# Row factors from transposed tiles, and first results held on chip, in a hybrid encoder layer

## The chip, the cores and the metric

The kernel runs on one core of a Trainium2 chip. The metric is the device time of one execution in microseconds; of several runs the median counts. The core has five engines that work side by side and wait for one another by semaphores: TensorE (PE in the profile, with its weight loads as PEld), VectorE (DVE), ScalarE (ACT), GpSimd (POOL) and SyncE (SP). SP issues nearly all DMA transfers in its program order; ACT and POOL issue a few.

## The reference, cut to what matters

```python
def hybrid_layer(x, w_in, w_out, norm_w, ...):          # x: 1 x 1024 x 2048, float32
    h = rms_norm(x, norm_w)                             # x * rsqrt(mean(x*x) + 1e-6) * norm_w, per token
    proj = h @ w_in                                     # 2048 x 6656
    rq, rk, rv, rg, aq, ak, av, ag = jnp.split(proj, splits, axis=-1)
    y_ret = retention_branch(rq, rk, rv, ...) * jax.nn.silu(rg)
    y_att = window_attention_branch(aq, ak, av, sink) * jax.nn.silu(ag)
    return x + jnp.concatenate([y_ret, y_att], axis=-1) @ w_out

def reference(...):
    return rms_norm(hybrid_layer(...), final_norm_w)
```

For the change only the beginning matters: `h = rms_norm(x)` and the first blocks of `h @ w_in`. The factor of a token needs the sum of squares over all 2048 columns of its row of `x`.

## The kernel before

**The projection.** All products are computed in a split form: each float32 operand is taken as a rounded high part and a remainder (`split`, `operand`, `low`: the high part is a cast on ScalarE, the remainder a subtraction on VectorE, line 86), and three matmuls (`mm3`, lines 100 to 102) make one product. The weights stand as stationary operands, 128 x 128; the transposed activations stream, 512 tokens at a time. `w_in` is worked off in blocks of 512 columns (`BLOCKS`), in two halves of the 2048 rows (`part` 0 and 1), in the order of `PHASES`. Inside a block with its 1024 rows of `w_in` the work is a two-by-two product of quarters in seven products instead of eight (`PRODUCTS`), whose operands are sums and differences of quarters: `w_next` and `mixed` make those of the weights, `sum_of` and `put` those of the activations, in `comb[i]`.

**The opening.** The first three blocks of part 0 are `akv`, `aq0` and `aq1`. They begin before the row factors are known. `plain` computes block `akv` with four ordinary quarters, first for token half 0 from `x` scaled by `norm_w` alone; then `early` computes one quarter of `aq0` and one of `aq1`, also for token half 0; then `plain` computes `akv` for token half 1, with factors; then `rest` does the remaining products of `aq0` and `aq1`. After that the ordinary loop goes on with `rk0`. The results that were made without factors, eight tiles of 128 x 512 (four from `plain`, two from each `early`), are stored unscaled to `pr` in HBM (lines 372 to 377 and 399 to 404) and noted in `unscaled`. The job `rescaled` (lines 1186 to 1196) later loads them back two at a time into `ct` buffers (line 1191), multiplies them by the row of factors (line 1194) and stores them again.

**The factors.** `src0` holds the transposed tiles of x's first 1024 columns, `[128, s, k, token]`, s = 0, 1 and k = 0 to 3, loaded by `load_first`. The squares don't use it: `load_rows` and `load_row_beside` load x's eight blocks of 128 rows in natural layout, 1 MiB each, and `square` sums the squares of half a row at a time, eleven halves on ScalarE (line 501) and five on VectorE (line 503). `factors_of` adds both halves and raises to the power -0.5 on POOL (line 510), `spread` repeats the result over 128 columns (line 1075), and `turn_rows` transposes that on TensorE (line 1079) and copies it into `both`, whose halves are `rows_of` (line 1080). `scale` multiplies a tile of `src0` by `norm_w` and that row (line 1084).

**What sets the order.** Each call of `advance` is a step: six matmuls are emitted, and then every running job moves on by one `yield`. Steps 1 to 16 are `plain` for token half 0, 17 to 24 `early` of `aq0`, 25 to 32 `early` of `aq1`, 33 to 48 `plain` for half 1, 49 to 68 `rest` of `aq0`, 69 to 88 `rest` of `aq1`, and `rk0` begins with step 89. The job `opening` performs what the dictionary `plan` lists for each step (`at(n, what, ...)`, lines 1131 to 1178). TensorE, SP and POOL keep program order throughout; up to step 66 (`BY_HAND`) the others do too, and afterwards a planner orders VectorE and ScalarE, except for what `behind` pins. `flush` sends the collected stores to SP at every fourth step. `keep` stores the operands of part 0 to HBM for a later phase, `second_part` loads and scales the transposed tiles of x's other 1024 columns into the buffer of `src0`.

**Buffers that matter.** `ct` is a ring of eight tiles of 128 x 512, used for every result between its bank and its store. `pj` and `ax` are four PSUM banks each. The tag `tt` has four tiles of 128 x 1024. The `a11` to `a22` tiles hold weight quarters, and `c1` to `c7` operands and, early on, natural rows.

Of the kernel before, what the change touches and what calls it, by code (L numbers as in the profile page):

```python
# [38 lines left out]
M = 4  # L39
# [20 lines left out]
def hybrid_layer_kernel(  # L60
# [293 lines left out]
    def plain(b, m, of, ops_):  # L354

        for n, k in QUARTERS:
# [5 lines left out]
            for q in range(M):  # L362
# [7 lines left out]
                if last:  # L370
                    for a in range(2):
                        e = ct()
                        nc.scalar.copy(out=e, in_=banks[a])
# [18 lines left out]
    def early(b):  # L392
# [84 lines left out]
    junk = st.tile([P, 2, PART], BF16, name="junk", tag="tt", bufs=4)  # L477
    ssx = st.tile([P, 2, NT], F32, name="ssx")
    natural = {}

    def load_rows(slot, *tokens):

        both = combp.tile([P, 2, 2, PART], F32, name="xt", tag=f"c{slot}")
        for i, t in enumerate(tokens):
            natural[t] = both[:, i, 0], both[:, i, 1]
            nc.sync.dma_start(out=both[:, i], in_=x[blk(t)].rearrange("p (h c) -> p h c", h=2))

    def load_row_beside(t):

        natural[t] = [st.tile([P, PART], F32, name="xh", tag="tt", bufs=4) for _ in range(2)]  # L490
        for i in range(2):
            nc.sync.dma_start(out=natural[t][i], in_=x[blk(t), i * PART:(i + 1) * PART])
# [4 lines left out]
    def square(t, i, act):  # L497

        of = natural[t][i]
        if act:  # L500
            nc.scalar.activation(out=junk[:, 0], in_=of, func=AF.Square, accum_out=ssx[:, i, t:t + 1])
        else:
            nc.vector.tensor_tensor_reduce(out=junk[:, 1], in0=of, in1=of, scale=1.0, scalar=0.0,
                                           op0=ALU.mult, op1=ALU.add, accum_out=ssx[:, i, t:t + 1])
# [544 lines left out]
    w_next[1, 1] = quarter(*u1, 1, 1)  # L1049
    load_rows(6, 4, 5)  # L1050
    w_next[1, 2] = quarter(*u1, 1, 2)
    load_rows(7, 6, 7)
    load_first(nc.sync, 0, 1)
    early_w = {1: st.tile([P, M, 2 * P], F32, name="b", tag="tt", bufs=4), 2: wp.tile([P, M, 2 * P], F32, name="s2", tag="s2")}

    def early_quarter(k):
        nc.sync.dma_start(out=early_w[k], in_=w_at((k - 1) * M, BLOCKS[u2[1]]))

    early_quarter(1)
    load_first(nc.sync, 1, 1)  # L1060

    def load_rest():
        load_rows(6, 0, 1)
        early_quarter(2)
        load_row_beside(2)
        for n in (2, 1), (2, 2):
            w_next[n] = quarter(*u1, *n)
# [18 lines left out]
    def hold_second():  # L1086
        t = combp.tile([P, 2, M, HALF], F32R, name="b12", tag="c7")
        quarters[1, 1] = t[:, 0], t[:, 1]
        hold(3, 0)
# [28 lines left out]

    mixed_first = mixed(w_next, then_of(1))
# [11 lines left out]
    at(6, lambda: ready.append(operand(w_next[1, 1])))  # L1131
    for n, t in ((9, 4), (11, 5), (14, 6), (16, 7)):
        at(n, square, t, 0, True)
        at(n, square, t, 1, False)
    at(12, load_rest)
    at(13, lambda: ready.append(operand(w_next[1, 2])))
    at(16, factors_of, 4, 8)
    at(17, spread, 1)
    at(20, lambda: turn_rows(1, first_banks[0, 2][0]))
    at(20, lambda: ready.append(operand(early_w[1])))  # L1140
    at(20, hold_second)
    at(20, second_half, 0, "scale")
    for k in range(2 * M):
        at(21 + k, second_half, k, "high")
        if k + 1 < 2 * M:
            at(21 + k, second_half, k + 1, "scale")
        at(21 + k, second_half, k, "low")
    for n, t, i in ((23, 0, 0), (24, 0, 1), (25, 1, 0), (25, 1, 1), (27, 2, 0), (28, 2, 1), (31, 3, 0)):
        at(n, square, t, i, True)
    at(25, lambda: ready.append(operand(early_w[2])))  # L1150
    at(26, load_rows, 6, 3)
    at(31, square, 3, 1, False)
    at(31, factors_of, 0, 4)
    at(33, spread, 0)
    for n in (29, 30, 32, 32, 34, 43, 51, 52, 56, 60):
        at(n, step)
    at(35, lambda: turn_rows(0, first_banks[u1[1], 2][0]))
    for k in range(M):
        at(36 + k // 2, scale, 0, k, 0)
    for j in range(2):  # L1160
        at(38 + j, sum_of, 5, j)
        at(40 + j, sum_of, 6, j)
        at(42 + j, put, 5, j)
        at(45 + j, put, 6, j)
        at(47 + j, sum_of, 7, j)
        at(48 + j, scale, 1, 2 * j, 0)
        at(48 + j, scale, 1, 2 * j + 1, 0)
        at(50 + j, put, 7, j)
        at(51 + j, sum_of, 4, j)
        at(54 + j, put, 4, j)  # L1170
        at(57 + j, put, 1, j)
        at(62 + j, put, 2, j)
    for n, i in ((40, 5), (43, 6), (48, 7), (52, 4)):
        at(n, hold, i, 0)
    at(41, first_scaled, u1[1])
    at(62, lambda: start(keep(0)))
    at(66, lambda: start(second_part()))
# [8 lines left out]
    def rescaled():  # L1186
# [463 lines left out]
```

## Time and profile before

| what | value |
|---|---|
| median of three runs | 1524.88 us (1523.79 to 1527.82) |
| profiled execution | 1520.95 us, its span 1519.1 us |
| mean granted TensorE clock | 0.993 |
| ScalarE busy | 670.6 us, 44% of the span |
| HBM read, written | 202.21 MB, 129.24 MB |
| DMA packets | 142228, 324.39 MB |

A row of the timeline gives start, duration, engine, source line, operation, output and inputs, the shapes, the count of merged instructions, and in brackets the idle time before the first of them with what ended it. Times are microseconds from the start of the span. `SPq` and `ACTq` are DMA issues: the duration is that of the issue, not of the transfer. A matmul's duration includes its way through the pipeline, so the distance of starts tells the rate. The granted clock is 1.00 at full speed.

### The profile page before, as it was taken

How to read it: one execution, taken by the hardware profiler on the slowest of the kernel's cores; microseconds unless marked ns; L12 is line 12 of the kernel's file. 1: busy time of each engine (PE TensorE's matmuls, PEld its weight loads, DVE VectorE, ACT ScalarE, POOL GpSimd, SP SyncE). 2: the span in 40 equal slices, each digit the busy share in tenths (PEclk: the TensorE clock that was granted, in tenths of full speed). 3: DMA queues.
4: the chain of work that ended last, by engine and by line, in shares of the span. 5: the costliest groups of instructions: out<-in, count | busy, mean ns of one | idle time of the engine just before them, and what ended most of it. 6: DMA issues, size and time to landing. Idle time of an engine off the chain costs nothing.

```text
span 1519.1 us, 19942 instructions
## 1 busy us (share of the span) xinstructions
PE 1485.2 (98%) x7096; PEld 1246.9 (82%) x7096; DVE 1117.3 (74%) x1932; ACT 670.6 (44%) x1091; POOL 149.2 (10%) x176
## 2 busy tenths in 40 slices
PE   9998999999999999999999999999999999999997
PEld 8777788888888888888888788887888878888886
DVE  4897595557858685867988899887655966776766
ACT  5531263234535453533434445354444663542425
POOL 0000001111110000001211100001211102020001
PEclk9999999999999999999999999999999999999999
DMA  9539776888675535798877766589787799495656
GB/s 372 182 121 390 251 249 187 227 223 251 165 235 195 169 123 190 273 339 185 176 185 167 176 178 187 172 293 325 224 233 194 175 210 211 90 205 175 211 179 250
DMA packets 142228, 324.39 MB, mean 214 GB/s; under 512 B 31664, under 2 KB 52528, under 8 KB 132400
## 3 DMA queue, kind: packets, MB, share of 16 engines
q1 hardware_dynamic: 118224, 272.23, 53.6%
q0 software_dynamic: 19728, 36.71, 16.4%
q10 hardware_dynamic: 4176, 14.17, 2.7%
q8 instruction: 56, 0.92, 0.2%
q14 instruction: 44, 0.36, 0.1%
HBM read 202.21 MB, written 129.24 MB: 218 GB/s over the span
## 4 chain that ended last, share of the span: by engine, by line
PE 75%; issue 9%; DMA 8%; DVE 5%; ACT 1%; POOL 1%; SPq 0%; ACTq 0%; POOLq 0%; DVEq 0%
PE pj L102 19%; PE pj L100 18%; PE pj L101 18%; PE ax L101 5%; PE ax L102 5%; PE ax L100 5%; PE ax L875 2%; PE ax L662 1%; DMA src<-in_x_f_dram 1%; DMA pr<-ct 1%; DVE wL L86 1%; DMA c<-kept 1%; DMA a<-in_w_in_dram 1%; DMA ysrc<-pr 1%; PE ax L926 1%
## 5 line engine op out<-in xcount | busy, mean ns | idle before, releaser
L100 PE MATMUL pj<-c,wH 128*128 128x512 f32 x1384 | 550.8, 398 | 10.7 <-DVE ct L93 5.3
L102 PE MATMUL pj<-c,wL 128*128 128x512 f32 x1384 | 543.9, 393 | 9.5 <-DVE wL L86 9.4
L101 PE MATMUL pj<-c,wH 128*128 128x512 f32 x1384 | 541.5, 391 | 0.0
L102 PEld LDWEIGHTS pj<-c,wL 128*128 128x128 f32 x1384 | 261.3, 189 | 70.1 <-DVE wL L86 14.6
L100 PEld LDWEIGHTS pj<-c,wH 128*128 128x128 f32 x1384 | 261.6, 189 | 61.9 <-issue 6.5
L101 PEld LDWEIGHTS pj<-c,wH 128*128 128x128 f32 x1384 | 261.7, 189 | 49.4
L86 DVE TENSOR_TENSOR wL<-a,wH 128x1024 fp32r<-128x1024 f32 x151 | 183.9, 1218 | 111.1 <-ACT wH L194 61.1
L194 ACT CAST wH<-a 128x1024 fp32r<-128x1024 f32 x121 | 127.1, 1050 | 181.6 <-PE pj L101 137.0
L336 ACT COPY ct<-pj 128x512 f32<-128x512 f32 x184 | 107.0, 586 | 191.9 <-PE pj L102 186.5
L93 DVE TENSOR_TENSOR ct<-pj,ct 128x512 f32<-128x512 f32 x170 | 112.6, 684 | 51.5 <-PE pj L102 42.1
L309 POOL DMA_DIRECT2D pr<-ct x88 | 78.1, 963 | 522.5 <-DVE ct L93 411.8
L86 DVE TENSOR_TENSOR wL<-s,wH 128x1024 fp32r<-128x1024 f32 x57 | 69.6, 1221 | 58.5 <-ACT wH L194 51.8
L101 PE MATMUL pj<-wL,c 128*128 128x512 f32 x224 | 87.3, 390 | 0.5 <-DVE wL L86 0.5
L102 PE MATMUL pj<-wH,c 128*128 128x512 f32 x224 | 87.2, 389 | 0.0
L100 PE MATMUL pj<-wH,c 128*128 128x512 f32 x224 | 87.1, 389 | 0.0
L101 PE MATMUL ax<-wL,c 128*128 128x512 f32 x208 | 81.2, 390 | 0.6 <-DVE wL L86 0.6
L102 PE MATMUL ax<-wH,c 128*128 128x512 f32 x208 | 81.0, 389 | 0.0
L100 PE MATMUL ax<-wH,c 128*128 128x512 f32 x208 | 80.9, 389 | 0.0
L194 ACT CAST wH<-s 128x1024 fp32r<-128x1024 f32 x51 | 53.6, 1051 | 16.2 <-PE pj L101 8.6
L89 ACT CAST wH<-a 128x1024 fp32r<-128x1024 f32 x28 | 29.5, 1054 | 62.1 <-PE pj L102 35.0
L652 ACT ACTIVATE s<-s,nm 128x385 f32<-128x385 f32 (+1 forms) x64 | 37.6, 588 | 30.1 <-DVE nm L647 27.2
L101 PEld LDWEIGHTS pj<-wL,c 128*128 128x128 f32 x224 | 42.0, 188 | 9.7 <-DVE wL L86 0.9
(227 smaller groups left out, 2121.0 us busy)
## 6 DMA issues: line engine op xcount, KB each, us to landing
a<-in_w_in_dram SPq DMA_DIRECT2D x103, 512.0 KB, 5.9
kept<-c SPq DMA_DIRECT2D x28, 1024.0 KB, 7.3
c<-kept SPq DMA_DIRECT2D x28, 1024.0 KB, 8.9
pr<-ct SPq DMA_DIRECT2D x96, 256.0 KB, 5.7
pr<-ct POOLq DMA_DIRECT2D x88, 256.0 KB, 5.9
a<-in_w_out_dram SPq DMA_DIRECT2D x18, 512.0 KB, 4.9
rx<-pr SPq DMA_DIRECT2D x64, 128.0 KB, 5.5
ysrc<-pr ACTq DMA_DIRECT2D x16, 512.0 KB, 6.4
```

The costliest lines, as they stand in the source:

```text
L86: return nc.vector.tensor_tensor(out=dst, in0=src, in1=high.bitcast(F32), op=ALU.subtract)
L89: behind(pinned, nc.scalar.copy(out=dst_h, in_=src))
L93: nc.vector.tensor_tensor(out=dst, in0=a, in1=b, op=ALU.add)
L100: nc.tensor.matmul(po, aH, bH, start=first, stop=False, **kw)
L101: nc.tensor.matmul(po, aH, bL, start=False, stop=False, **kw)
L102: nc.tensor.matmul(po, aL, bH, start=False, stop=last, **kw)
L194: behind(pinned, nc.scalar.copy(out=wH, in_=src))
L309: nc.gpsimd.dma_start(out=dst, in_=t, accum_op=ALU.add)
L336: nc.scalar.copy(out=t, in_=bank)
L652: nc.scalar.activation(out=s[:, 0:w + 1], in_=s[:, 0:w + 1], func=AF.Exp, scale=-1.0, bias=nm, accum_out=den)
L662: nc.tensor.transpose(pt[:, blk(j)], s[:, blk(j)], ident)
L875: nc.tensor.matmul(p, k_tok[:, c // 2, :, c % 2], vd[:, c, d], start=True, stop=True)
```

## The change

- **First loads.** The first piece of `src0` goes to SP's queue as its first transfer and the small vectors become the first on ACT's; both halves of the first weight quarter are on SP.
- **Squares of the first 1024 columns** come from `src0`. `square_columns` squares two 512-wide tiles at a time on ScalarE into the four `tt` tiles, `add_columns` sums them on VectorE, and `sum_columns` sums over the partitions with eight matmuls of one column against a tile of ones, then copies four columns of sums to `ssx`.
- **Squares of the other 1024 columns** still come from natural rows, of which only that half is loaded now (`load_row`, 512 KB each); all eight are on ScalarE (`square_row`), in steps 13 to 22.
- **Results without factors** stay in their `ct` buffers. `scale_result` multiplies two at a time in steps 28, 31, 37 and 48 and hands them to the stores. The first store, the load back and the second store of `rescaled` are gone.
- **The plan** is shifted: the factors of token half 0 are made in step 23 instead of 31 and turned in step 26 instead of 35; the early weight quarters use the tags `a21` and `a22`, so the two quarters of `aq0` that belong there are loaded in steps 21 and 25; operands 7, 4 and 2 are placed later; `second_part` starts in step 69 instead of 66.

The diff, cut to its core:

```diff
@@ plain, early @@
-                        stores.append((True, to, e))
-                        if m == 0:
-                            unscaled.append(to)
+                        (unscaled if m == 0 else stores).append((True, to, e))
...
-            stores.append((True, to, e))
-            unscaled.append(to)
+            unscaled.append((True, to, e))
@@ squares @@
-    junk = st.tile([P, 2, PART], BF16, name="junk", tag="tt", bufs=4)
+    junk = wp.tile([P, PART], BF16, name="junk", tag="ct", bufs=8)
+    columns = [st.tile([P, 2, HALF], F32, name="xx", tag="tt", bufs=4) for _ in range(4)]
...
+    def load_row(t):
+        nc.sync.dma_start(out=natural[t], in_=x[blk(t), PART:])
...
+    def square_row(t):
+        nc.scalar.activation(out=junk, in_=natural[t], func=AF.Square, accum_out=ssx[:, 1, t:t + 1])
+
+    def square_columns(m, i):
+
+        s, j = divmod(i, 2)
+        nc.scalar.activation(out=columns[(m, 2, 3, 2)[i]], in_=src0[:, s, 2 * j:2 * j + 2, half(m)], func=AF.Square)
+
+    def add_columns(m, i):
+        acc = columns[m]
+        if i < 4:
+            add(acc, acc, columns[(m, 2, 3, 2)[i]])
         else:
...
+            add(acc[:, 0], acc[:, 0], acc[:, 1])
+
+    def sum_columns(m, pt):
+
+        for t in range(4):
+            nc.tensor.matmul(pt[:, t:t + 1], columns[m][:, 0, blk(t)], ones, start=True, stop=True)
+        nc.vector.tensor_copy(out=ssx[:, 0, 4 * m:4 * m + 4], in_=pt[:, 0:4])
@@ first loads @@
+    load_first(nc.sync, 0, 0, 0, 1)
+    nc.scalar.dma_start(out=vec_t, in_=vecs)
     half_of_a11(nc.sync, 0)
-    load_first(nc.scalar, 0, 0, 0, 1)
-    nc.scalar.dma_start(out=vec_t, in_=vecs)
     load_first(nc.sync, 0, 0, 1, 1)
-    half_of_a11(nc.scalar, 2)
+    half_of_a11(nc.sync, 2)
...
+    def early_quarter(k):
+        t = early_w[k] = wp.tile([P, M, 2 * P], F32, name="b", tag=f"a2{k}")
+        nc.sync.dma_start(out=t, in_=w_at((k - 1) * M, BLOCKS[u2[1]]))
...
+    load_quarter(1, 1)
     load_first(nc.sync, 0, 1)
...
+    load_first(nc.sync, 1, 1)
+    for t in (4, 5, 6, 7):
+        load_row(t)
+    load_quarter(1, 2)
+    load_row(0)
+    load_row(1)
     early_quarter(1)
...
+    load_row(2)
+    load_row(3)
+    early_quarter(2)
@@ plan @@
+    def scale_result(n=2):
+        for _ in range(n):
+            _, to, e = unscaled.pop(0)
+            nc.vector.tensor_tensor(out=e, in0=e, in1=rows_of[0], op=ALU.mult)
+            stores.append((True, to, e))
...
+    for n, m in ((8, 0), (11, 1)):
+        at(n, square_columns, m, 0)
+        at(n, square_columns, m, 1)
+        for i in (1, 2, 3):
+            at(n + i, add_columns, m, i)
+            if i < 3:
+                at(n + i, square_columns, m, i + 1)
+        at(n + 3, add_columns, m, 4)
+    at(13, lambda: sum_columns(0, first_banks[0, 1][0]))
+    for n, t in ((13, 4), (14, 5), (15, 6), (15, 7), (18, 0), (19, 1), (21, 2), (22, 3)):
+        at(n, square_row, t)
+    at(16, lambda: sum_columns(1, first_banks[0, 1][1]))
     at(16, factors_of, 4, 8)
+    at(16, lambda: ready.append(operand(w_next[1, 2])))
+    at(16, spread, 1)
+    at(19, lambda: turn_rows(1, first_banks[0, 2][0]))
...
+    at(21, load_quarter, 2, 1)
...
+    at(23, factors_of, 0, 4)
+    at(24, spread, 0)
+    at(24, lambda: ready.append(operand(early_w[2])))
+    at(25, load_quarter, 2, 2)
+    at(26, lambda: turn_rows(0, first_banks[u1[1], 2][0]))
+    at(28, scale_result)
+    at(31, scale_result)
+    at(37, scale_result)
+    at(48, scale_result)
...
-    at(66, lambda: start(second_part()))
+    at(69, lambda: start(second_part()))
...
-    def rescaled():
-        yield from idle(74)
-        for i in range(0, len(unscaled), 2):
-            es = [ct() for _ in range(2)]
-            for e, of in zip(es, unscaled[i:i + 2]):
-                nc.sync.dma_start(out=e, in_=of)
-            yield from idle(7)
-            for e, of in zip(es, unscaled[i:i + 2]):
-                nc.vector.tensor_tensor(out=e, in0=e, in1=rows_of[0], op=ALU.mult)
-                stores.append((True, of, e))
-            yield from idle(7)
```

More of the change, by code (lines that the diff above doesn't have):

```diff
@@ L488, in load_row_beside, with load_natural @@
[L488 to L492, printed above, removed]
+    natural = []
+    ones = st.tile([P, 1], F32, name="ones")
+    nc.vector.memset(ones, 1.0)
+    def load_natural(slot):
+        t = combp.tile([P, 4, PART], F32, name="xt", tag=f"c{slot}")
+        return [t[:, i] for i in range(4)]
+    def load_row(t):
+        nc.sync.dma_start(out=natural[t], in_=x[blk(t), PART:])
@@ L1129, in at @@
         plan.setdefault(n, []).append((what, args))
[L1131 to L1136, printed above, removed]
-    at(16, factors_of, 4, 8)
-    at(17, spread, 1)
-    at(20, lambda: turn_rows(1, first_banks[0, 2][0]))
+    at(7, lambda: ready.append(operand(w_next[1, 1])))
+    for n, m in ((8, 0), (11, 1)):
[6 more added lines that the diff above has]
+        at(n + 3, add_columns, m, 4)
@@ L1142, in hybrid_layer_kernel @@
-    at(20, second_half, 0, "scale")
+    at(21, load_quarter, 2, 1)
+    at(23, hold_third)
     for k in range(2 * M):
-        at(21 + k, second_half, k, "high")
+        at(20 + k, second_half, k, "high")
         if k + 1 < 2 * M:
[L1146 to L1155, printed above, removed]
+            at(20 + k, second_half, k + 1, "scale")
+        at(20 + k, second_half, k, "low")
+    at(23, factors_of, 0, 4)
[5 more added lines that the diff above has]
+    at(31, scale_result)
@@ L1156, in hybrid_layer_kernel @@
+    at(37, scale_result)
+    at(48, scale_result)
+    for k in range(M):
+        at(33 + k // 2, scale, 0, k, 0)
+    for n in (29, 30, 40, 40, 42, 47, 51):
         at(n, step)
-    at(35, lambda: turn_rows(0, first_banks[u1[1], 2][0]))
-    for k in range(M):
-        at(36 + k // 2, scale, 0, k, 0)
     for j in range(2):
-        at(38 + j, sum_of, 5, j)
-        at(40 + j, sum_of, 6, j)
-        at(42 + j, put, 5, j)
+        at(35 + j, sum_of, 5, j)
+        at(38 + j, sum_of, 6, j)
+        at(40 + j, put, 5, j)
@@ L1164, in hybrid_layer_kernel @@
         at(45 + j, put, 6, j)
[L1165 to L1175, printed above, removed]
+        at(49 + j, sum_of, 7, j)
+        at(51 + 2 * j, put, 7, j)
+    for n, i in ((40, 5), (45, 6), (51, 7)):
+        plan[n].insert(0, (hold, (i, 0)))
@@ L1176, in hybrid_layer_kernel @@
+    at(44, first_scaled, u1[1])
+    at(52, step)
+    at(56, step)
+    for j in range(2):
+        at(54 + j, scale, 1, 2 * j, 0)
+        at(54 + j, scale, 1, 2 * j + 1, 0)
+        at(57 + j, sum_of, 4, j)
+    at(59, hold, 4, 0)
+    at(59, put, 4, 0)
+    at(60, step)
+    at(61, put, 4, 1)
+    for j in range(2):
+        at(62 + j, put, 1, j)
+        at(66 + j, put, 2, j)
     at(62, lambda: start(keep(0)))
-    at(66, lambda: start(second_part()))
+    at(69, lambda: start(second_part()))
@@ L1184, in opening @@
             yield
[L1186 to L1199 removed]
+    start(opening())
     to_load = deque()
```

36 lines of the change are left out of this document (7 added, 29 removed).

## The prediction

> **What bounds the kernel now.** I read the page first, then the windows, then the TensorE rows of the timeline that carry an idle time, and last the other engines' rows at those places. The page's first lines:
>
> ```profile
> span 1519.1 us, 19942 instructions
> PE 1485.2 (98%) x7096; PEld 1246.9 (82%) x7096; DVE 1117.3 (74%) x1932; ACT 670.6 (44%) x1091; POOL 149.2 (10%) x176
> ```
>
> TensorE is the bound on average, so the change is worth what TensorE loses where the change reaches: the first 200 us. These are its large waits there, from the timeline:
>
> ```profile
> 50.19 0.50 PE L100 MATMUL pj<-c,wH 128*128 128x512 f32 x1 [2.71 <-ACT wH L194]
> 51.45 0.78 PE L102 MATMUL pj<-c,wL 128*128 128x512 f32 x1 [0.53 <-DVE wL L86]
> 59.50 3.71 PE L369 MATMUL pj<-b,w 128*128 128x512 f32 x15 [0.47 <-DVE ct L93]
> 103.68 0.47 PE L100 MATMUL pj<-c,wH 128*128 128x512 f32 x1 [0.56 <-DVE ct L93]
> 129.31 0.47 PE L100 MATMUL pj<-c,wH 128*128 128x512 f32 x1 [3.24 <-DVE ct L93]
> 138.19 0.47 PE L100 MATMUL pj<-c,wH 128*128 128x512 f32 x1 [1.54 <-DVE ct L93]
> 175.40 0.79 PE L102 MATMUL pj<-c,wL 128*128 128x512 f32 x1 [3.34 <-DVE wL L86]
> ```
>
> The windows around them (busy time and count of each engine, granted clock, DMA share, GB/s):
>
> ```profile
> 52.00:59.00 7.00, 7.00 (x25) 5.34 (x23) 6.47 (x11) 6.36 (x11) 0.11 (x1) 0.79 0.50 181
> 66.00:102.00 36.00, 36.00 (x160) 29.82 (x159) 36.00 (x39) 17.83 (x20) 0.00 (x0) 1.00 0.25 77
> 126.00:140.00 14.00, 9.22 (x33) 7.10 (x33) 11.21 (x14) 1.99 (x2) 0.00 (x0) 0.88 1.02 417
> 175.00:182.00 7.00, 6.60 (x17) 5.21 (x18) 2.08 (x3) 0.00 (x0) 0.00 (x0) 0.56 0.67 215
> ```
>
> Undisturbed, a matmul takes 36.00/159 = 0.226 us and a step of six 1.36. Each wait of 2.7 us or more is followed by a lower granted clock: it costs 7 x 0.21 = 1.5 us near 52, 14 x 0.12 = 1.7 near 130, 7 x 0.44 = 3.1 near 178. [...] From 66 to 102 VectorE is busy 36.00 of 36.00 us, so there it is as much a bound as TensorE.
>
> Why the two late waits exist, from the VectorE and SP rows:
>
> ```profile
> 113.69 1.11 SPq L307 DMA_DIRECT2D pr<-ct  x2
> 122.80 0.83 SPq L1191 DMA_DIRECT2D ct<-pr  x2
> 130.42 5.04 SPq L307 DMA_DIRECT2D pr<-ct  x4
> 128.48 2.52 DVE L93 TENSOR_TENSOR ct<-pj,ct 128x512 f32<-128x512 f32 x4 [0.28 <-DMA pr<-ct]
> 171.02 1.37 DVE L93 TENSOR_TENSOR ct<-pj,ct 128x512 f32<-128x512 f32 x2 [5.65 <-issue]
> 173.52 0.69 DVE L1194 TENSOR_TENSOR ct<-ct,rows 128x512 f32<-128x512 f32 x1 [1.12 <-DMA ct<-pr]
> 174.12 1.22 DVE L86 TENSOR_TENSOR wL<-s,wH 128x1024 fp32r<-128x1024 f32 x1
> ```
>
> At 128 the evictions wait for a `ct` buffer: two of the eight are held by the re-read of L1191, and the next free one waits for a store issued by 114.8 that lands only near 128.4, in a queue whose DMA share is 1.02. At 172 VectorE takes L1194, which waits 1.12 us for its re-read, ahead of the `wL` on which TensorE is waiting.
>
> **The change, part by part.** Prices come from these rows; where rows are merged I divide to the next start.
>
> ```profile
> 1.18 5.98 DMA vec_t<-in_vecs_dram
> 16.85 18.77 DMA src<-in_x_f_dram
> 19.63 1.07 ACT L373 COPY ct<-pj 128x512 f32<-128x512 f32 x2 [1.72 <-PE pj L369]
> 20.59 1.07 ACT L501 ACTIVATE junk<-xt 128x1024 bf16<-128x1024 f32 x1
> 21.55 0.20 ACT L501 ACTIVATION_READ_ACCUMULATOR junk<-xt 128x1 f32 x1
> 72.91 2.94 ACT L89 CAST c<-tt 128x1024 fp32r<-128x1024 f32 x3
> 39.33 1.41 DVE L1084 SCALAR_TENSOR_TENSOR src<-src,vec_t,rows 128x512 f32<-128x512 f32 x2
> 57.31 1.22 DVE L503 CUSTOM_DVE_ANT_0 junk<-xt 128x1024 bf16<-128x1024 f32 x1
> 58.46 0.08 DVE L503 DVE_READ_ACCUMULATOR2_ANT ssx<- 128x1 f32 x1
> 58.76 1.29 DVE L93 TENSOR_TENSOR ct<-pj,ct 128x512 f32<-128x512 f32 x2
> 64.31 2.74 DVE L1084 SCALAR_TENSOR_TENSOR src<-src,vec_t,rows 128x512 f32<-128x512 f32 x4 [1.66 <-ACT rows L1080]
> 66.96 2.35 DVE L96 TENSOR_TENSOR tt<-src 128x1024 f32<-128x1024 f32 x2
> 69.23 2.35 DVE L96 TENSOR_TENSOR tt<-src,tt 128x1024 f32<-128x1024 f32 x2
> 108.65 1.21 DVE L86 TENSOR_TENSOR wL<-a,wH 128x1024 fp32r<-128x1024 f32 x1
> 1.36 6.57 PE L1028 MATMUL pj<-ident 128*128 128x128 f32 x32 [1.36 <-POOL ident masks.py:199]
> 63.05 0.60 PE L1079 MATMUL pj<-ident,factors 128*128 128x128 f32 x4
> 61.09 0.42 DVE L1075 COPY factors<-rms 128x512 f32<-128x512 f32 x1
> 32.91 1.03 POOL L510 TENSOR_TENSOR rms<-rms,neg_half 128x4 f32<-128x4 f32 x1 [31.60 <-DVE rms L509]
> a<-in_w_in_dram SPq DMA_DIRECT2D x103, 512.0 KB, 5.9
> ```
>
> ScalarE: 0.95 for a 1024-wide cast (2.94/3) and, I assume, for a square without accumulator; 1.18 for one with it; 0.5 for a 512-wide copy. VectorE: 1.135 for any 1024-wide add or subtraction ((69.23 - 66.96)/2), 0.66 for a scaling ((66.96 - 64.31)/4), 0.6 for 512-wide work.
>
> Start: `vec_t` goes from second to first on its queue, 0.44 us earlier by the issue times; the bounds are 0 and 0.44, I take 0.4, because it is the start of the chain.
>
> Loads: of x half is left, 4 MiB, and eight stores and eight re-reads of 256 KB go. Up to the last early weight the queue carries the same 7.5 MiB as now (two x tiles 2, eight half rows 4, three weights 1.5; now rows 4, tiles 2, weights 1, two stores 0.5), which take 18.77 us, 2.5 us per MiB: rows 4 to 7 arrive by 27, rows 2 and 3 by 34.4, the last weight by 35.6. None of it is awaited, as the next lines show; a load that came late would cost its delay beyond 2 us for rows 4 to 7, 6 for rows 2 and 3.
>
> Squares, to the first factor row. ScalarE is in order, so the column squares start behind the copies after step 8, at 19.63 - 0.4 = 19.2. Copies to 20.2; squares of token half 0 at 0.95, with VectorE's adds taking turns on the shared scratch: the last full add ends at 25.65, the short one at 26.25; half 1 likewise at 30.8. Then the square of four rows on ScalarE (from 28.9, 4 x 1.18) to 33.6, two copies to 34.55, the weight cast to 35.5, its `wL` 36.7, the spread 37.05, two more row squares, the row copy 38.35; POOL's 1.03 lies beside the cast and `wL`, and in the second round beside the evictions. Scaling of the second half starts at 38.4, against 39.33 now.
>
> TensorE meanwhile gets eight plain f32 matmuls of one column. The trace has none: L1028 shows two records for each f32 matmul, 6.57/32 = 0.205 each with 128 columns, so sixteen cost at most 3.3 us; at the transposes' 0.60/4 = 0.15 for eight they cost at least 1.2. They can't be a gain. I take 2.0, nearer the transposes because only one column streams. Step 14 starts at 19.2 + 5 x 1.36 = 26.0, so the first sum waits 0.2; the second finds its data. Step 20 is reached at 36.4, waits 0.6 for the spread, and step 27 at 47.0.
>
> VectorE from 38.4: the scalings 0 to 4 (3.3), remainders 0 to 3 (2.4), `wL` of the first early weight (1.135), the factors' sum (0.15), two evictions (1.2), scaling and remainder 5 and 4 (1.25), spread (0.35), and 0.3 for ScalarE between: 48.5. So the transposes after step 26 wait 1.5 us, a new wait, too short, I take it, to lower the clock (waits of 0.5 did not lower it, 2.71 did; if 1.5 does, it costs 1.5 more, as near 52). The old one of 2.71 goes: `wL` of the second early weight is ready at 49.6, TensorE wants it near 52. On SP the load of the last quarter, moved behind that `wL` because it takes its buffer, is issued at 49.6 and lands 5.9 later at 55.5; its reader is reached near 55.2, and only held results' stores stand behind it on SP: 0.3 at most. Step 33 starts at 48.9 + 6 x 1.36 = 57.0.
>
> VectorE from 48.5 to the last of what precedes step 53: eighteen 1024-wide operations (20.4), twelve 512-wide adds and products, the eight held results among them (7.2), six scalings (4.0), three remainders (1.8): 81.9. TensorE reaches step 53 at 57.0 + 20 x 1.36 = 84.2, so VectorE waits there. Then four pairs of evictions (4.8), fourteen 1024-wide (15.9) and four scalings (2.65) to the `wL` of the second early block: 107.6, against 108.65 + 1.21 = 109.9 now. TensorE wants it at 106.5 and waits 1.1. **Gain up to here 2.3 us.** The held results' products cost nothing beyond this sum only while `ct` buffers turn over: eight, with nine wanted once; the ninth takes the scratch of the squares, free by then. The results' stores are issued once scaled, between 54 and 82, with DMA share 0.25 around them, before the evictions that reuse them at 68 to 90.
>
> Later: without L1191 the evictions at 128 find two more buffers, so 3.24 + 1.54 + 1.7 = **6.5 us** come back. At 172, without L1194, `wL` follows the eviction of 171.02 directly: 1.12 + 0.60 earlier, a wait of 1.6 instead of 3.34, too short for the clock: 1.7 + 3.1 = **4.8 us**. Second-part loads and its puts move three to four steps (4 to 5 us) later; VectorE's pinned work on them has slack, since it idles 5.65 us before 171. If that cover is gone, it costs that shift.
>
> Sum: 2.3 + 6.5 + 4.8 = 13.6. The profiled execution took 1520.95 (span 1519.1 and 1.85 around it), the median of the runs is 3.93 higher; 1520.95 - 13.6 = 1507.3 in a profile, 1524.88 - 13.6 = **1511.3** as median.
>
> **The rivals.** *One late wait stays.* From step 66 on VectorE's order is chosen by the planner and not by hand; the pattern at 172 can return elsewhere. Then 1524.88 - 8.8 = 1516.1. For it: `wL` stood behind an eviction even before L1194.
>
> *Hidden anyway.* The second-part tiles and the kept operands, 1 MiB each, fill the queue alone, stores land as late as now, and both waits stay: 1524.88 - 2.3 = 1522.6. For it the share of 1.02; against it that two buffers are freed whatever the queue does.
>
> *Slower: VectorE becomes the bound.* It gains eight adds (8.0) and, ahead of step 53, eight products (4.8) and loses five squares of 1.22 + 0.08 (6.5): 6.3 more before 109.9, in a stretch that shows 36.00 of 36.00. If the idle time before 54 doesn't absorb it, the second early block starts 6.3 later and the crowd of second-part loads moves with it, so nothing comes back: 1531.2. It decides where that `wL` ends after 109.9. Against it: VectorE now waits for ScalarE and DMA through the first squares.
>
> *Short loads.* Slices of the first loads:
>
> ```profile
> GB/s 0 45 182 193 213 345 411 424 406 393 393 404 414 418 418 418 430 418 451 385 397 442 406 426 418 403 387 391 387 410 387 393 387 418 436 455 404 418 414 418
> ```
>
> At the 193 GB/s of the fourth microsecond the 7.5 MiB would take 41 us, rows 2 and 3 land near 55, and step 26 would wait some 10 us more and lose 1.7 of clock: 1523.0. [...]
>
> **How the numbers follow.** About 0.3%, 4.6 us, is what a measurement here can tell from no change. Forecast 0.52, its own range 1505 to 1516 (down by the new waits, 1.5 + 0.6 + 1.1, sums at 1.2 and the 1.6 at 172, which makes 1505.7; up by a lowered clock at two of them, 1.5 + 1.7, and sums at 3.3, which makes 1515.8); one late wait stays 0.17; hidden anyway 0.14; short loads 0.05; slower 0.12. Faster 0.69, within 0.19, slower 0.12. The range 1505 to 1523.5 leaves out the slower case and a few hundredths below.
>
> **What would show it.** Right: no L1191 or L1194; HBM reads down by 6 MiB and writes by 2; `rows` of the first half copied near 50 instead of just before 64.31; short waits after steps 19 and 26 with the clock at 1.00; the second early block's `wL` near 107.6; no wait over 2 us at 126 to 182. Wrong: that `wL` after 109.9, a clock below 0.9 before 60, or an eviction waiting for a store.

## The result, and the profile after

| what | before | after |
|---|---|---|
| median of 4 runs each | 1524.34 us (1521.97 to 1527.82) | 1515.05 us (1513.79 to 1515.38) |
| ratio, 95% interval | | 0.9936 (0.9915 to 0.9956) |
| profiled execution, its span | 1520.95, 1519.1 us | 1515.38, 1513.5 us |

The kernel became faster by 9.3 us of median, inside the range of 1505.0 to 1523.5 and 3.75 us above the 1511.3 forecast. The two profiles lie only 5.6 us apart, because the profiled execution of before (1520.95) was faster than all four of its timed runs, and that of after the slowest of its own. Three rows of the page of after:

```profile
span 1513.5 us, 19947 instructions
PE 1484.5 (98%) x7112; PEld 1247.4 (82%) x7112; DVE 1122.6 (74%) x1933; ACT 675.2 (45%) x1093; POOL 149.0 (10%) x176
HBM read 195.92 MB, written 127.14 MB: 213 GB/s over the span
```

TensorE has sixteen records more (the column sums), and HBM traffic fell by 6.29 MB read and 2.10 MB written, as the diff says: 4 MiB of x, and 2 MiB each of re-reads and of first stores. TensorE's busy time did not change (1484.5 us, 1485.2 before). So the gain is again in what TensorE waits. Its waits in the first 200 us, from the timeline of after:

```profile
25.58 1.02 PE L510 MATMUL pj<-ones,xx 128*128 128x1 f32 x8 [0.78 <-DVE xx L93]
36.38 0.63 PE L1089 MATMUL pj<-ident,factors 128*128 128x128 f32 x4 [0.53 <-DVE factors L1085]
48.50 1.02 PE L1089 MATMUL pj<-ident,factors 128*128 128x128 f32 x4 [1.93 <-DVE factors L1085]
105.69 0.47 PE L100 MATMUL pj<-c,wH 128*128 128x512 f32 x1 [3.23 <-DVE ct L93]
135.85 0.47 PE L100 MATMUL pj<-c,wH 128*128 128x512 f32 x1 [1.08 <-DVE ct L93]
```

The waits of 2.71 (at 50), 3.24 (at 129) and 3.34 (at 175) are gone and the one of 1.54 (at 138) fell to 1.08. New are 0.78, 0.53 and 1.93 in the chain of the factors, and **3.23 at 105.69, where before had 0.56**. The windows of after at these places (the fourth is the 126 to 140 of the prediction):

```profile
46.00:53.00 7.00, 5.07 (x18) 3.91 (x17) 6.91 (x12) 3.29 (x6) 0.81 (x1) 0.76 0.27 76
66.00:102.00 36.00, 36.00 (x160) 29.81 (x159) 32.91 (x36) 18.97 (x21) 0.00 (x0) 1.00 0.32 102
104.00:112.00 8.00, 6.31 (x21) 5.06 (x22) 8.00 (x9) 1.05 (x1) 0.00 (x0) 0.79 0.59 236
126.00:140.00 14.00, 12.92 (x57) 10.43 (x56) 10.38 (x12) 2.10 (x2) 0.00 (x0) 1.00 1.02 424
165.00:182.00 17.00, 17.00 (x77) 14.08 (x76) 8.17 (x12) 4.24 (x6) 0.00 (x0) 1.00 0.91 329
```

The clock is now lowered near 50 (0.76) and 107 (0.79) and full at 126 to 182. The DMA share at 126 is 1.02 as before: the queue is as full, and still the evictions no longer wait for it. A ledger says what each place is worth: the start of the same step on TensorE in both traces. A negative difference is a lead of after. (Where a wait is given "between starts", here and below, it is the distance of the starts of two neighbouring matmuls less the undisturbed 0.23 us; the figure in a row's brackets is the idle time alone.)

| step | before | after | difference | what lies between |
|---|---|---|---|---|
| 1 | 8.17 | 6.33 | -1.84 | the start |
| 13 | 25.10 | 23.28 | -1.82 | |
| 17 | 30.54 | 31.48 | +0.95 | two column sums and their wait |
| 27 | 44.60 | 49.17 | +4.56 | both turns of factors, lowered clock |
| 33 | 58.19 | 58.78 | +0.59 | the 2.71 of before is gone |
| 61 | 97.52 | 96.86 | -0.67 | |
| 65 | 103.68 | 105.69 | +2.01 | the new wait |
| 70 | 110.95 | 114.21 | +3.26 | lowered clock behind it |
| 85 | 138.19 | 135.85 | -2.33 | evictions at 129 and 138 no longer wait |
| 113 | 183.25 | 174.02 | -9.23 | the wait at 175 and its clock are gone |
| 170 | 261.50 | 251.91 | -9.59 | |
| last | 1509.10 | 1504.15 | -4.95 | lost at 273, 846 and 1235 |

The whole opening, up to step 70, lost 3.26 us; the prediction had it gain 2.3. Everything that was won came later. These are the rows of VectorE and ScalarE behind the new wait:

```profile
69.18 1.27 ACT L373 COPY ct<-pj 128x512 f32<-128x512 f32 x2 [15.05 <-PE pj L369]
72.37 2.36 DVE L86 TENSOR_TENSOR c<-tt,c 128x1024 fp32r<-128x1024 f32 x2 [3.09 <-ACT c L89]
86.13 1.29 DVE L93 TENSOR_TENSOR ct<-pj,ct 128x512 f32<-128x512 f32 x2
92.24 1.29 DVE L93 TENSOR_TENSOR ct<-pj,ct 128x512 f32<-128x512 f32 x2
102.58 2.37 DVE L86 TENSOR_TENSOR c<-src,c 128x1024 fp32r<-128x1024 f32 x2
104.85 1.29 DVE L93 TENSOR_TENSOR ct<-pj,ct 128x512 f32<-128x512 f32 x2
111.19 1.23 DVE L86 TENSOR_TENSOR wL<-a,wH 128x1024 fp32r<-128x1024 f32 x1
```

The eviction at 104.85 is that of the product made in steps 61 to 64. Steps 65 to 68 write the same two banks, so TensorE stands until the first half of that eviction is through. Ahead of it on VectorE stand the two remainders at 102.58, of operand 1, which no step needs yet. The `wL` of the second early block ends at 111.19 + 1.23 = 112.4.

The order alone is not new. In before two remainders, those of operand 2, stand ahead of the same eviction, and TensorE waits 0.56 for it:

```profile
93.65 1.28 DVE L93 TENSOR_TENSOR ct<-pj,ct 128x512 f32<-128x512 f32 x2
100.58 2.35 DVE L86 TENSOR_TENSOR c<-src,c 128x1024 fp32r<-128x1024 f32 x2
102.85 1.28 DVE L93 TENSOR_TENSOR ct<-pj,ct 128x512 f32<-128x512 f32 x2
```

What grew is the work in this stretch. From the eviction of the product of steps 53 to 56 (product 6) to that of steps 61 to 64 (product 7) VectorE works without a pause for 9.20 us in before (93.65 to 102.85) and for 12.61 in after (92.24 to 104.85), while TensorE's eight steps take 10.9 (8 x 1.36). Among it are seven 1024-wide operations that make operands (four for operand 4, which the change placed later, one for operand 2, two for operand 1) where before had four.

### The profile page after: what moved, and what is told of

Same layout as the page of the kernel before. It is cut to its first block, busy times and chain, and to the rows that moved or that the text cites. A ratio compares the mean times of both kernels' runs of the same rounds, so it can differ in the third digit from the quotient of the medians.

```text
span 1513.5 us, 19947 instructions
## 1 busy us (share of the span) xinstructions
PE 1484.5 (98%) x7112; PEld 1247.4 (82%) x7112; DVE 1122.6 (74%) x1933; ACT 675.2 (45%) x1093; POOL 149.0 (10%) x176
## 4 chain that ended last, share of the span: by engine, by line
PE 86%; DVE 5%; DMA 4%; issue 2%; ACT 1%; SPq 1%; POOL 1%; POOLq 0%; DVEq 0%; ACTq 0%
PE pj L102 22%; PE pj L100 22%; PE pj L101 22%; PE ax L101 5%; PE ax L102 5%; PE ax L100 5%; PE ax L882 2%; PE pj L369 1%; DMA pr<-ct 1%; PE ax L669 1%; DVE wL L86 1%; DMA yt<-mix 1%; PE ax L852 1%; DVE c L86 1%; PE ax L933 1%
## 5 line engine op out<-in xcount | busy, mean ns | idle before, releaser
L100 PEld LDWEIGHTS pj<-wH,c 128*128 128x128 f32 x224 | 42.5, 190 | 10.7 <-ACT wH L89 1.8
```

What stands on the lines that cost most here:

```text
L100: nc.tensor.matmul(po, aH, bH, start=first, stop=False, **kw)
```

## The experiments

Every expectation names its theories by letters and says what each holds. Ledgers below are against the before of the table above, by the start of the same step.

**Holding alone.** Before, with its eight unscaled results kept in `ct`; squares and loads as they were.

```diff
-            stores.append((True, to, e))
-            unscaled.append(to)
+            unscaled.append((True, to, e))
...
-    at(41, first_scaled, u1[1])
+    for n in (35, 37, 39, 46):
+        at(n, scale_result)
+    at(44, first_scaled, u1[1])
...
-    for job in (opening(), rescaled()):
+    for job in (opening(),):
```

> The kernel before with one part of the change: the eight first results stay in their ct buffers and are multiplied after steps 35, 37, 39 and 46; the re-read and the second store are gone; squares, loads and second_part are as before. Theory H (the gain is the waits that the re-reads caused): the waits of 3.2 us at step 81, 1.5 at step 85 and 3.3 in step 109 go, the opening up to step 69 loses at most the 4.8 us of eight products that now lie in the stretch where VectorE is full; 1514 to 1520 us. Rival L (the gain is the lighter load queue: half of x's rows, earlier start): 1524 us and the three waits stay. Rival S (the gain is second_part starting three steps later): 1524 us and the waits stay.

Measured: 1523.34 us (1518.34 to 1524.41), ratio 0.9974 (0.996 to 0.9987). Of its waits on TensorE two bear on this:

```profile
108.02 0.47 PE L100 MATMUL pj<-c,wH 128*128 128x512 f32 x1 [2.29 <-DVE ct L93]
146.25 0.50 PE L102 MATMUL pj<-c,wL 128*128 128x512 f32 x1 [2.66 <-DVE wL L86]
```

The waits of 3.24 at 129 and 3.34 at 175 are gone here too, so the missing re-read ended them. But step 65 is 4.34 late (the eight products come on top of VectorE's unchanged squares), and a new wait of 2.66 stands at 146. VectorE is late here ahead of the place: it begins the eviction of the product of steps 49 to 52 at 92.16, 5.8 us after that product's last matmul. Steps 93 and 113 stand at +3.81 and -3.08. Holding alone brings a quarter per cent. The expected 1514 to 1520 us were missed: by the time alone the rivals with their 1524 come closer, and only the waits, which both rivals had staying, tell theory H from them.

**The change without holding.** The reverse: after, with results stored, re-read and stored again.

```diff
-            unscaled.append((True, to, e))
+            stores.append((True, to, e))
+            unscaled.append(to)
...
-    at(28, scale_result)
-    at(31, scale_result)
-    at(37, scale_result)
-    at(48, scale_result)
...
+    for job in (opening(), rescaled()):
+        start(job)
```

> The changed kernel with holding alone undone: the first results are stored unscaled, loaded back and stored again as before the change; column squares, half rows and the later second_part stay. Theory H: long waits return between steps 77 and 113, 5 to 11 us, while the wait at step 65 shrinks because eight products (4.8 us of VectorE) leave the opening; 1518 to 1524 us. Rivals L and S: no such waits, 1510 to 1515 us.

Measured: 1529.75 us (1524.32 to 1533.06), ratio 1.0019 (1.0004 to 1.0034): slower than before, and 13 to 16 us slower than after. The rivals that expected 1510 to 1515 here fell, but theory H's 1518 to 1524 was missed too, by some 6 us, and the wait at step 65, which was to shrink without the eight products, is still 2.99. The two late waits are back, with the cause in VectorE's rows:

```profile
133.48 0.47 PE L100 MATMUL pj<-c,wH 128*128 128x512 f32 x1 [2.86 <-DVE ct L93]
180.00 0.80 PE L102 MATMUL pj<-c,wL 128*128 128x512 f32 x1 [3.56 <-DVE wL L86]
178.12 0.69 DVE L1229 TENSOR_TENSOR ct<-ct,rows 128x512 f32<-128x512 f32 x1 [1.34 <-DMA ct<-pr]
178.73 1.22 DVE L86 TENSOR_TENSOR wL<-s,wH 128x1024 fp32r<-128x1024 f32 x1
```

L1229 is the product after the re-read, as L1194 was in before: VectorE takes it, waits 1.34 for its load, and only then makes the `wL` that TensorE wants. With the experiment above this shows that the two late waits hang on the re-read; the rest of the change without holding brings a loss of 0.2%.

**Second part three steps earlier**, as in before; all else as after.

```diff
-    at(69, lambda: start(second_part()))
+    at(66, lambda: start(second_part()))
```

> The changed kernel with second_part started in step 66 as before the change. Theory H (the late waits went with the re-reads): no wait over 2 us at steps 81 to 113, the end within 2 us of the changed kernel's. Rival S (they went because the second-part loads came three steps later): waits of 3 us at steps 81 or 109 return, 5 us or more.

Measured, one run: 1523.19. Up to step 85 the ledger is within 2 us of after's, then step 93 stands at +3.80 where after has -2.34. The chain in this kernel's rows, SP's issues first:

```profile
113.71 0.43 SPq L543 DMA_DIRECT2D src<-in_x_t_dram  x1
116.55 1.35 SPq L543 DMA_DIRECT2D src<-in_x_t_dram  x2
118.00 1.48 SPq L307 DMA_DIRECT2D pr<-ct  x2
134.40 0.33 SPq L201 DMA_DIRECT2D a<-in_w_in_dram  x1
126.22 1.29 DVE L93 TENSOR_TENSOR ct<-pj,ct 128x512 f32<-128x512 f32 x2 [3.62 <-DMA pr<-ct]
140.57 1.05 ACT L194 CAST wH<-a 128x1024 fp32r<-128x1024 f32 x1 [8.40 <-DMA a<-in_w_in_dram]
144.99 1.22 DVE L86 TENSOR_TENSOR wL<-a,wH 128x1024 fp32r<-128x1024 f32 x1
146.26 0.67 PE L102 MATMUL pj<-c,wL 128*128 128x512 f32 x1 [2.66 <-DVE wL L86]
```

Three loads of the second part stand ahead of the stores of 118.00, the first of them (113.71) also ahead of the two stores before; in after the first two loads are issued at 115.30, behind that first pair of stores. The eviction at 126.22 waits 3.62 for a store to land; the weight load at 134.40 comes late, its cast waits 8.40 for it, and so on to TensorE. It is the wait that holding alone showed at 146.25. So the theory that the place of the second part costs nothing was wrong: between steps 85 and 93 alone it is worth 4.5 us. The rival that priced it expected another wait.

**The first loads as before.**

```diff
-    load_first(nc.sync, 0, 0, 0, 1)
-    nc.scalar.dma_start(out=vec_t, in_=vecs)
     half_of_a11(nc.sync, 0)
+    load_first(nc.scalar, 0, 0, 0, 1)
+    nc.scalar.dma_start(out=vec_t, in_=vecs)
     load_first(nc.sync, 0, 0, 1, 1)
-    half_of_a11(nc.sync, 2)
+    half_of_a11(nc.scalar, 2)
```

> The changed kernel with the first five loads in the order and on the queues of before. If the earlier start (first matmul of the projection at 6.33 instead of 8.16 us) comes from the order of the first loads: it goes back to 8.0 to 8.3, and steps 2 to 13 are 1.8 us later. If it comes from anything else in the load queue: it stays at 6.3. The end moves less than the start where a VectorE wait follows.

Measured, one run: 1517.74; the first product starts at 7.78, 1.44 later than in after. But the start scatters: over the eleven traces with the new order it lies at 6.33 to 7.88 (mean 7.14), over the three with the old one (before, holding alone, this) at 7.78 to 8.17 (mean 7.96). The new order is worth some 0.8 us, and a single pair of traces can't size it. From step 29 this kernel even leads after by 0.3 us: the wait of 2.1 after step 26 was not followed by a lowered clock here (the matmuls behind it, from 50.53 on, start 0.22 to 0.24 us apart).

**No column squares.** This kernel leaves out the squares of x's first 1024 columns and their sums, and puts a constant in their place.

```diff
-        at(n, square_columns, m, 0)
-        at(n, square_columns, m, 1)
...
-    at(13, lambda: sum_columns(0, first_banks[0, 1][0]))
+    at(8, lambda: nc.vector.memset(ssx[:, 0], float(PART)))
...
-    at(16, lambda: sum_columns(1, first_banks[0, 1][1]))
```

> The changed kernel with the squares of x's first 1024 columns left out: no column squares on ScalarE, no adds on VectorE, no column sums on TensorE; that part of the sums is set to a constant. Theory V (up to step 69 VectorE's queue from step 40 on sets the time): steps 14 to 33 come 3 to 6 us earlier, but step 69 by less than 2, since the wait at step 65 grows. Rival C (the column squares themselves cost what was lost): step 69 comes 4 to 6 us earlier too.

Measured, one run: 1512.84. Step 9 starts 1.27 later than in after (the start), steps 20 to 113 some 2.35 earlier: the sums cost about 3.6 on the path. The wait at 105 is 3.40 between starts as in after, and the shift passes through it unchanged. The theory that this wait absorbs what is saved ahead of it fell: it moves along with TensorE. Rival C was right about the way and too high with its 4 to 6 us.

**The turn two steps later.**

```diff
-    at(26, lambda: turn_rows(0, first_banks[u1[1], 2][0]))
+    at(28, lambda: turn_rows(0, first_banks[u1[1], 2][0]))
```

> The changed kernel with the transposes of the first half's factors after step 28 instead of 26. The wait of 2.09 us for the spread goes, and with it the lowered clock behind it (1.5): step 33 comes 3 to 3.6 us earlier. By theory P the shift stays to the end, since the plan of steps 53 to 64 moves along with TensorE. Rival V: the wait at step 65 grows by the same 3 us and step 69 stays at 112.9.

Measured, one run: 1513.24. The wait of 1.93 and the clock behind it are gone:

```profile
46.00:53.00 7.00, 7.00 (x34) 5.83 (x33) 7.00 (x12) 3.51 (x6) 1.02 (x1) 1.00 0.20 51
```

TensorE is busy 7.00 of 7.00 at full clock, where after had 5.07 at 0.76. With a start 0.95 later, steps 29 to 170 are 2.8 earlier than in after, so the two steps were worth 3.7. The wait at 105 again stays 3.40.

**Other work into VectorE's gap at 69 to 72.** Two kernels, each with a piece of work that stands ahead of step 65 moved to step 39: the difference for operand 7, or the four scalings of steps 54 and 55.

```diff
+        at(39, sum_of, 7, j)
...
-        at(49 + j, sum_of, 7, j)
```

> The changed kernel with the two subtractions of sum 7 moved from steps 49 and 50 to step 39, into the 3.09 us in which VectorE waits for ScalarE (69.28 to 72.37). Theory P (the wait of 3.4 us at step 65 is made by the 18.7 us of VectorE work that the plan puts between the evictions of products 5 and 7, which start together with TensorE at step 53): the gap shrinks by 2.3, VectorE idles that much before step 53 instead, and the wait at step 65 stays 3.2 to 3.5. Rival V (one full queue from step 40 to 69): the wait shrinks by 2.3 to about 1.1 and its lowered clock goes; step 69 comes 3 to 4 us earlier.

```diff
+    for k in range(M):
+        at(39, scale, 1, k, 0)
...
-        at(54 + j, scale, 1, 2 * j, 0)
-        at(54 + j, scale, 1, 2 * j + 1, 0)
```

> The changed kernel with the four scalings of the second quarter (2.65 us) moved from steps 54 and 55, behind the eviction of product 5, to step 39. Theory P: the wait at step 65 falls by 2.65 to 0.6 to 0.9 and the lowered clock behind it (1.6) goes; step 70 comes about 4 us earlier than in the changed kernel and the end too, if no later wait takes it. Rival V: the same, since this fills the gap as well; so it is told from P only together with the run before it.

Measured, one run each: 1517.18 and 1514.35. The first leaves 3.15 (between starts) at step 65 and a new 0.95 at 69, the second leaves 2.48 where 0.6 to 0.9 was expected. In both VectorE is now on time at an earlier eviction, where it waits for TensorE, at step 53 in the first and at step 57 in the second:

```profile
84.35 1.37 DVE L93 TENSOR_TENSOR ct<-pj,ct 128x512 f32<-128x512 f32 x2 [1.56 <-PE pj L102]
91.31 1.37 DVE L93 TENSOR_TENSOR ct<-pj,ct 128x512 f32<-128x512 f32 x2 [0.50 <-PE pj L102]
```

So the wait at step 65 doesn't come from VectorE being late up to there. In the second kernel VectorE works 13.02 us from this eviction of product 6 to that of product 7 (91.31 to 104.33). The planner had used the gap for one remainder of operand 2 as well and left the other one in this stretch. So the remainders of operand 2 were pinned behind step 66, alone and with the two moves above:

```diff
-        split(*(comb[i][:, hl, 2 * j:2 * j + 2] for hl in range(2)), of)
+        split(*(comb[i][:, hl, 2 * j:2 * j + 2] for hl in range(2)), of, i == 2)
```

> The changed kernel with only the splits of operand 2 pinned. Theory P: one 1024-wide subtraction (1.135) less between the evictions of products 5 and 7: the wait at step 65 falls from 3.4 to 2.2 or 2.3. Rival V: it stays 3.4, or what it loses comes back as a wait at step 69.

> The changed kernel with three moves: the transposes of the first half's factors after step 28 instead of 26; the scalings of the second quarter at step 39 instead of 54 and 55; the splits of operand 2 pinned, so that the planner can't take them ahead of step 66. Theory P: VectorE has 15.6 us between the evictions of products 5 and 7 (three evictions of 1.2, ten 1024-wide operations of 1.135, one product of 0.6), less than TensorE's 16.3, so the wait at step 65 is under 0.3, and the wait for the spread at step 26 is gone with its lowered clock: step 70 comes 7 to 9 us earlier than in the changed kernel, and 1505 to 1509 us at the end if no later wait takes it. Rival V (VectorE's total up to step 69 is the bound): at most the 2.8 us of the later turn; 1512 us.

Measured: 1513.39 (one run) with 2.85 at step 65, and 1514.02 (1513.58 to 1516.94; ratio 0.9917, 0.9901 to 0.9933) with 3.18. Both missed: the second was to leave less than 0.3. In the second the eviction of product 7 did come 3.02 earlier than in after (101.83 for 104.85), but the later turn had brought TensorE 2.8 earlier as well, so the wait stayed. Rival V, which gave the kernel at most these 2.8, came nearest: step 70 starts 3.0 earlier than in after. Its rows:

```profile
89.67 1.38 DVE L93 TENSOR_TENSOR ct<-pj,ct 128x512 f32<-128x512 f32 x2 [0.43 <-issue]
99.56 2.36 DVE L86 TENSOR_TENSOR c<-src,c 128x1024 fp32r<-128x1024 f32 x2
101.83 1.28 DVE L93 TENSOR_TENSOR ct<-pj,ct 128x512 f32<-128x512 f32 x2
102.66 0.58 PE L100 MATMUL pj<-c,wH 128*128 128x512 f32 x1 [3.01 <-DVE ct L93]
```

The order is as in after: two remainders of operand 1, then the eviction. From the eviction of product 6 at 89.67 VectorE works without a pause for 12.16 us up to that of product 7, with TensorE's eight steps at 10.9. (The 0.43 us of idle time ahead of 89.67 are no wait for TensorE: the last matmul of product 6 ends at 88.77. The profile doesn't show what ended them.) Of the 12.16 the two remainders are 2.27, and no step needs them yet.

**After again**, measured together with the last two.

> The changed kernel itself, as the measure for the run before it on the same chip: 1513 to 1516 us. If its clock falls at other waits than in the first profile, then the half-speed stretches behind waits of 2 to 3 us are a matter of phase, and this profile's step times differ from the first one's by 1.4 to 1.7 us at such a place and by the start of the first loads.

Measured: 1514.22 (1509.99 to 1518.36), ratio 0.9914 (0.9893 to 0.9935). The three moves can't be told from it.

**Operand 1 behind the eviction.** The three moves, and:

```diff
-        at(62 + j, put, 1, j)
+        at(64 + j, put, 1, j)
```

> The kernel of the three moves (its wait at step 65 was 3.18 us, step 70 at 111.16) with one edit more: the two splits of operand 1 (put 1) go from steps 62 and 63 to 64 and 65, which in VectorE's order puts 2.27 us of work behind the eviction of product 7, for which step 65 waits. Theory O (the order alone is the fault: work that nobody needs yet stands ahead of the eviction): the eviction starts 2.3 earlier, the wait at step 65 falls to 0.6 to 1.2, nothing comes back, and step 70 starts 2 to 3.5 earlier than with the three moves (the half-clock stretch behind the wait goes too). Theory B (VectorE's total work between step 53 and step 69 is the bound, and the rival 'VectorE becomes the bound' was right about the place): the wait at step 65 falls just the same, but the wL for step 69 still ends at about 108.4 to 109, so that step 69 waits 2.5 to 3.2 and step 70 starts within 0.7 of 111.2. Time by O: 1 to 3 us under the three moves at step 129; by B: equal to them. At the end of the kernel either is expected to lose a part of its lead at 1230 to 1240, where the kernels that led by 10 to 12 us at 1153 all led by only 4 to 7 afterwards, as x's loads for the last products come no earlier.

Measured: 1508.81 us (1507.90 to 1511.88), ratio 0.9895 (0.9875 to 0.9915). The rows that stood above, in this kernel:

```profile
89.12 1.32 DVE L93 TENSOR_TENSOR ct<-pj,ct 128x512 f32<-128x512 f32 x2 [0.34 <-issue]
98.97 1.28 DVE L93 TENSOR_TENSOR ct<-pj,ct 128x512 f32<-128x512 f32 x2
100.17 1.22 DVE L86 TENSOR_TENSOR c<-src,c 128x1024 fp32r<-128x1024 f32 x1
105.90 1.22 DVE L86 TENSOR_TENSOR wL<-a,wH 128x1024 fp32r<-128x1024 f32 x1
99.80 0.47 PE L100 MATMUL pj<-c,wH 128*128 128x512 f32 x1 [0.59 <-DVE ct L93]
107.17 0.50 PE L102 MATMUL pj<-c,wL 128*128 128x512 f32 x1 [0.97 <-DVE wL L86]
```

The wait fell from 3.01 to 0.59, 0.97 came back at step 69, and step 70 starts at 108.21 instead of 111.16. Between the evictions of products 6 and 7 VectorE now has 9.85 us (89.12 to 98.97), less than TensorE's 10.9, and the wait is what it was in before (0.56). The 0.97 is what VectorE's amount of work up to this `wL` still costs. Its `wL` ends at 107.1, before the 109.9 of the old kernel. The median is 5.4 us under that of after again, which was taken on another chip; by the ratios to before the two are 2.9 us apart. Of after's ten timed runs one lies within this kernel's five, and the intervals of the two ratios overlap, so against after the gain is likely and not settled. The move alone, without the other three, was not run.

The expectation had the lead shrink near 1235 and gave a reason; the lead did shrink, from 13.1 at 1139 to 8.6 at 1418. The reason doesn't hold: the kernel without holding, which trails by 9.4, loses 3.0 over the same stretch, and the one without column squares, which leads by 6.7, loses nothing. What after shows there:

```profile
1231.88 1.06 ACT L1391 ACTIVATE ysrc<-ysrc 128x1024 f32<-128x1024 f32 x1 [4.58 <-DMA ysrc<-pr]
1234.90 0.50 PE L100 MATMUL pj<-wH,c 128*128 128x512 f32 x1 [1.42 <-ACT wH L89]
DMA  9698999999899999829998999999999999999768
```

ScalarE waits 4.58 for a load of `ysrc`, TensorE 1.42 for ScalarE, and the DMA engines' busy tenths from 1201 to 1245 are nearly all nines. This is a stretch paced by transfers, whose waits differ from one execution to the next (0.65 in before, 1.58 + 1.03 between starts in after). In after a lowered clock (0.76 from 1234 to 1241) takes 1.5 us more.

## Why the prediction was right, and where it was wrong

**Right: where the gain comes from.** The re-read was named as the cause of both late waits, and undoing the holding brought both back. By the ledger they gave 5.6 us (steps 77 to 85: +3.26 to -2.33; forecast 6.5, but 1.08 of the wait at 138 stayed) and 6.4 us (steps 109 to 113: -2.86 to -9.23; forecast 4.8, where a wait of 1.6 was left that did not come). Together 12.0 against 11.3. The rivals "one late wait stays" and "hidden anyway" are out; the row with a DMA share of 1.02 in both kernels shows why the second was wrong: the queue stayed full, but with two buffers more in the ring no eviction had to wait for it. "Short loads" is out as well: no wait for a row tile appears on the path, and from 7 to 33 us the loads of after, half rows of 512 KB among them, ran at 375 to 442 GB/s.

**Right: the small new costs.** Two column sums with their waits cost 2.8 us on TensorE's ledger (-1.82 to +0.95), 0.94 of it the first wait; forecast 2.0 and 0.2. Leaving them out gave 3.6. The wait at step 19/20 is 0.69 between starts (forecast 0.6). The old wait of 2.71 is gone.

**Wrong in size: the start.** Forecast 0.4, with bounds 0 to 0.44 taken from issue times. The pair shows 1.84, the means of all traces 0.8; about 1 us of the pair's lead was luck. The bounds left out that the first product's start varies by over a microsecond between traces.

**Wrong: "too short, I take it, to lower the clock".** The wait after step 26 was 2.09 between starts, not 1.5, and the clock fell behind it in this profile (0.76 from 46 to 53). The price for that case stood in the text (1.5 us more). Moving the turn by two steps gave the whole of it back, 3.7 us.

**Wrong: the sum from 48.5 to the second early block.** This is the step that failed. It said that VectorE, without a pause, is ahead of TensorE at step 53, "so VectorE waits there", and that the only price is 1.1 at step 69. VectorE did pause: ScalarE, in order, stood 15.05 us for the copies after step 40 (row 69.18), and VectorE's next operands came only behind those copies, at 72.37, after 3.09 idle, so that it reached the eviction of step 53 at 86.13 without a wait. But this is not what made the new wait: in the kernel with sum 7 moved and in the one without holding VectorE did wait for TensorE at step 53 (1.56 and 0.49 us), and step 65 still waited 2.99 in both. What failed is that the sum asked only when the last item of VectorE's list is done, not when the banks come free on the way. Steps 65 to 68 take the banks of steps 61 to 64, and in the 10.9 us that TensorE takes for steps 57 to 64 VectorE had 12.6 us of work from the eviction of product 6 to that of product 7. This is the wait of 3.23. In the order of the plan the sum's own prices put that eviction close to 101.8 with step 65 due at 100.5, and the sum charged TensorE nothing. Forecast at step 70 -2.3, measured +3.26. The sign that the text named for "wrong", that `wL` after 109.9, is there, at 112.4, and so is a clock below 0.9 before 60 (0.76); but the mishap did not take the later gains with it, as the rival "VectorE becomes the bound" had it. That rival had the place right and the consequence wrong: VectorE's amount of work accounts for 0.97 there once the order is mended.

**Wrong: the later second part "has slack, since it idles 5.65 us before 171".** It is no shift with slack. It keeps its first loads behind a pair of stores, and three steps earlier the kernel loses some 4.5 us between steps 85 and 93; holding alone, with the second part as early, has the same wait. The gain of the whole needs the two together.

**The end.** The sum took the lead at step 89 and after as final. Steps 113 to 170 lead by 9.2 to 9.9 us, the last matmul by 4.95: 1.7 lost between 273 and 314, 1.3 behind a lowered clock at 847, 2.6 near 1235 of which 0.6 had been won shortly before. None of these places is touched by the diff. Near 1235 twelve of the thirteen other traces lose 1.7 to 5.0 us against before, with the re-read as without it. Together with the medians, 9.3 apart (12.4 in the second measurement, where before had 1526.57), this speaks for a lucky profile of before; there is only one, so it is not shown.

So the time came out inside the range partly by luck: the opening went the other way by 5.6 us, and two of the signs named for "wrong" were seen. The late gains, which carried the forecast, are not luck.

## What to carry to other kernels

When a result is kept on chip instead of being stored and fetched again, look for the gain where the fetched buffers and their waits stood, which may be a hundred microseconds later than the code that changed. When a sum moves an engine close to its bound, don't add up its list to the end only: for each reuse of a bank or a buffer compare when the releasing instruction starts, in the engine's order, with when the next writer is due. For a wait of this kind the work between two evictions counts: with 12.1 to 13.0 us of it, where TensorE needs 10.9, the wait stayed at 2.3 to 3.2 us whatever was moved ahead of the first eviction; with 2.3 us put behind the second, 9.9 were left and the wait was 0.6.

## What the runs showed of the hardware

The clock behind a wait is not a matter of the wait's length alone. The same waits in two executions of the same kernel, after and after again (1.93 and 1.94 at 48 to 50, 3.23 in both at 105), in the windows of both:

```profile
47.00:52.00 5.00, 3.50 (x11) 2.93 (x12) 5.00 (x8) 2.19 (x4) 0.00 (x0) 0.67 0.29 69
103.00:110.00 7.00, 4.31 (x12) 3.49 (x13) 7.00 (x8) 0.34 (x1) 0.00 (x0) 0.76 0.76 287
845.00:851.00 6.00, 3.84 (x10) 2.78 (x11) 6.00 (x9) 3.97 (x8) 0.28 (x1) 0.72 0.73 130
```

```profile
47.00:52.00 5.00, 3.06 (x17) 2.27 (x16) 5.00 (x9) 2.14 (x5) 0.97 (x1) 1.00 0.11 17
103.00:110.00 7.00, 4.75 (x21) 3.99 (x22) 7.00 (x8) 0.79 (x1) 0.00 (x0) 1.00 0.72 288
```

The clock is 0.67 and 0.76 in the one and 1.00 in the other. Likewise the wait of 2.78 between starts near 850 is the same in before and after, and only after's is followed by a lowered clock (0.72 above); before had full speed:

```profile
853.00:859.00 6.00, 3.94 (x20) 3.07 (x21) 6.00 (x9) 3.97 (x7) 0.19 (x1) 1.00 0.63 127
```

Between the layer's first and last matmul every lowered stretch of before and after stands at 0.50 in windows of half a microsecond. By the windows at its edges it lasts some 3.4 us (51.5 to 54.9 and 130.0 to 133.4 in before, 48.7 to 52.1, 106.7 to 110.1, 847.4 to 850.8 and 1236.5 to 1239.9 in after) or, once, 6.8 (174.4 to 181.2 in before). No trace shows what decides whether a wait is followed by such a stretch; the phase that the expectation for after again names is not shown. So a wait of 2 to 3.4 us had a price of itself here, and in some executions one to two microseconds more (3.1 for the longer stretch near 178 in before), and two profiles of one kernel can differ by several of these.
